# A two-layer decoder trunk: attention scores in plain fp32 on two halves of the array

## The chip, the core and the metric

The kernel runs on one core of one Trainium2 chip. The core has TensorE (matrix products; PE in the profile, its weight loads PEld), VectorE (DVE), ScalarE (ACT), GpSimd (POOL) and SyncE (SP), which here only issues DMAs. The engines run side by side, each through its own list of instructions, and wait for each other through semaphores. The metric is the device time of one execution in microseconds (us).

## The reference, cut to what matters

256 positions of width 1024 go through two layers. Layer 0 has three groups of heads of width 64 that read one input projection: sparse attention (8 heads, 2 key groups; compressed blocks, selected blocks and a window, mixed by gates), block attention (8 heads) and attention into 256 memory tokens (4 heads). Layer 1 has retention (4 heads) and again memory attention. Each group is gated, the groups are joined, projected back and added to the residual; a norm ends it. With 256 positions the selected blocks, the window and the block attention all come to plain causal attention:

```python
s = einsum('bqhd,bshd->bhqs', q, k) * HEAD_DIM ** -0.5
p = masked_softmax(s, causal)
o = einsum('bhqs,bshd->bqhd', p, v)
# compressed blocks: 15 per key group, each from 32 positions
hid = silu(einsum('bnlgd,lde->bnge', blocks + pe, w1))
kc_or_vc = einsum('bnge,ef->bngf', hid, w2)
```

## The kernel before, in words

Nearly all time goes into projections (`project`, `project_turned`, `project_mem`, `out_project`). Each weight slice of 128 x 1024 is loaded into a "raw" buffer and split by `split` (L102) into a high part (ScalarE, L106, type float32r) and the rest (VectorE, L107); the activations are split as well, and `mm3` adds three float32r products, L119 to L121.

Attention works on pairs of heads, hh = 0 and 1. The channels of the two heads lie on the partitions 0 to 63 and 64 to 127. For the scores, `stack_q` (L311) puts the high part of a head's queries on one half of the partitions and the rest on the other half, and `stack_k` (L318) does the like for keys with the high part on both halves (`dst`) and the rest on both halves (`lo`). `scores` then needs two float32r products over all 128 rows for one head (L372, L373). The scores lie in two PSUM banks "s" (`BANKS`, L25).

`causal_pair` (L398) does the softmax: VectorE adds the mask and takes the maximum (L405), ScalarE the exponential (L407), the sums are inverted and applied, TensorE transposes the probabilities (L178), ScalarE copies them to `pt` (L419). The value products are plain fp32: head hh writes the column half 64 hh to 64 hh + 63 of the bank `o`, first 256 columns for the first 128 keys (L421), then 128 columns for the rest (L423). `mem_attention` (L439) is the same with 256 memory keys and four products of 256 columns (L469). The profile shows each plain fp32 product as two records, each with its weight load. There are four sparse pairs with two branches each, four block pairs, and two memory attentions of two pairs.

In `compress` (L494) keys and values go one after the other through a hidden layer (16 products of 30 columns each, L530) that fills one column half. In `sparse_pair` (L577) the compressed values start the sum `o` with two products of 15 rows (L585).

The order on each engine comes from a scheduler that places instructions by priority as soon as, by its own estimate, their inputs and a buffer are there; the program gives the priority by its order. Buffers with one tag share a fixed number of slots: `tl("v4", shape, NV)` is one of 12 slots of 4 KB per partition. A tile gets a slot when an earlier tile with the tag has been read for the last time; where the slot is taken over, its first writer waits for that reader. In the last projection (`out_project(5, ys, True)`, L695) the four last weight slices are "late": their eight halves go into "v4" slots (L708) and are held until all five sums (four of 512, 512, 512 and 256 columns in "pj" and "tr", and `rest` of 256 in "s") have taken them in. At that time `x0` holds two "v4" slots (L725) and `gf` one (L837). The end (from L841) adds the residual to each sum (L854, L851), squares it (ScalarE, L856), multiplies by the gain (L858, L862), scales (L865, L866) and writes the output (L867, L868).

Of the kernel before, what the change touches and what calls it, by code (L numbers as in the profile page):

```python
# [21 lines left out]
NV = 12  # L22
# [29 lines left out]
def trunk(  # L52
# [33 lines left out]
    def load(t, src):  # L86
        nc.sync.dma_start(t, src)
        return t

# [221 lines left out]
    def stack_q(dst, src):  # L311

        for i in range(2):
            own, other = slice(64 * i, 64 * i + 64), slice(64 - 64 * i, 128 - 64 * i)
            S.copy(dst[own, :, i], src[own])
            V.tensor_tensor(dst[other, :, i], src[own], dst[own, :, i].bitcast(F32), ALU.subtract)

    def stack_k(dst, lo, src):  # L318

        for i in range(2):  # L320
            own, other = slice(64 * i, 64 * i + 64), slice(64 - 64 * i, 128 - 64 * i)
            S.copy(dst[own, :, i], src[own])
            V.tensor_copy(dst[other, :, i], dst[own, :, i].bitcast(F32))
            V.tensor_tensor(lo[own, :, i], src[own], dst[own, :, i].bitcast(F32), ALU.subtract)
            G.tensor_copy(lo[other, :, i], lo[own, :, i].bitcast(F32))

    def mem_query(ps, rb, dst):
        e = tl("tmp2", [P, 512], 3).rearrange("p (k t) -> p k t", k=2)
        scaled(ps, rb, 0.125, e)
        stack_q(dst, e)  # L330
# [13 lines left out]
    def heads_q(ps, plain=None):  # L344

        dst = [tl("v4", [P, 2, 2, T], NV, F32R) for _ in range(2)]

        def done(b, ts):
            for i in range(2):
                stack_q(dst[i][:, :, :, ts], b[:, 2 * i : 2 * i + 2])  # L350
            if plain is not None:
                S.copy(plain[:, :, ts], b)

        rot_transpose(ps, "q", done)
        return dst

    def heads_k(ps):
        dst = [tl("v4", [P, 2, 2, T], NV, F32R) for _ in range(2)]
        lo = [tl("v4", [P, 2, 2, T], NV, F32R) for _ in range(2)]

        def done(b, ts):
            for i in range(2):
                stack_k(dst[i][:, :, :, ts], lo[i][:, :, :, ts], b[:, 2 * i : 2 * i + 2])

        rot_transpose(ps, "k", done)
        return dst, lo
# [8 lines left out]
    def pair_scores(q, k, kl):  # L375

        out = []
        for hh in range(2):
            s = bank("s")
            for tok, a in enumerate(SPAN):  # L380
                scores(s[:, a], q[:, hh, tok * P : (tok + 1) * P], k[:, hh, : a.stop - a.start], kl[:, hh, : a.stop - a.start])
            out.append([s[:, a] for a in SPAN])
        return out

    def branch_scores(q, k, kl):


        s0 = bank("s").rearrange("p (h b n) -> p h b n", h=2, b=2)
        got = [[[None, None], [None, None]] for _ in range(2)]
        for hh in range(2):  # L390
            scores(s0[:, hh], q[:, hh, 0:P], k[:, hh, :, 0:P], kl[:, hh, :, 0:P])
            s1 = bank("s").rearrange("p (b n) -> p b n", b=2)
            scores(s1, q[:, hh, P:T], k[:, hh], kl[:, hh])
            for br in range(2):
                got[br][hh] = [s0[:, hh, br], s1[:, br]]
        return got

    def causal_pair(ss, v, gate, o, first, last):  # L398
# [11 lines left out]
        for hh in range(2):  # L410
# [8 lines left out]
            S.copy(pt[:, hh, :384], transposes([p[:, hh, i * P : (i + 1) * P] for i in range(3)]))  # L419
        for hh in range(2):  # L420
            PE.matmul(o[hh * 64 : hh * 64 + 64, 0:T], v(hh, 0), pt[:, hh, 0:T], start=first, stop=False)  # L421
        for hh in range(2):
            PE.matmul(o[hh * 64 : hh * 64 + 64, P:T], v(hh, 1), pt[:, hh, T : T + P], start=False, stop=last)  # L423
# [8 lines left out]
    def mem_keys(ps, rstd, rb, kT, kl, v):  # L432
        e = tl("tmp2", [P, 512], 3).rearrange("p (k t) -> p k t", k=2)
        scaled(ps[0], rb, 1.0, e)
        stack_k(kT, kl, e)
# [3 lines left out]
    def mem_attention(eqT, kT, kl, v, szT, y):  # L439
        for pr in range(2):  # L440
# [4 lines left out]
            sm = tl("sm", [P, 2, 2], 3)  # L445
            for hh in range(2):
                s = bank("s")
                for tok in range(2):
                    a, qs = slice(tok * T, (tok + 1) * T), slice(tok * P, (tok + 1) * P)
                    scores(s[:, a], eqT[:, pr, hh, qs], kT[:, pr, hh], kl[:, pr, hh])  # L450
# [38 lines left out]
    def sparse_queries():  # L489
        nonlocal qT, nq  # L490
        qT = tl("v4", [P, 4, T], NV)
        nq = heads_q(project(w512, W["nq"], (xh, xl)), qT)
# [144 lines left out]
    def block_queries():  # L637
        nonlocal mq
        mq = heads_q(project(w512, W["mq"], (xh, xl)))
# [331 lines left out]
```

## Time and profile before

| what | us |
|---|---|
| median of three runs | 450.48 (450.01 to 451.08) |
| the profiled execution, its own time | 450.25 |
| its span, first to last instruction | 448.5 |
| TensorE busy | 435.9 |
| VectorE busy | 331.7 |
| ScalarE busy | 257.3 |
| GpSimd busy | 9.4 |

The span is what the profile shows; the time of the execution is 1.8 us longer. "Busy" of TensorE counts an instruction from its start to its modelled end, and instructions overlap: a product of 512 columns has a length of 0.39 us and is followed by the next after 0.23. For prices one therefore reads the step from one start to the next. L178 is the transposes' line, L119 to L121 are the projections'.

### The profile page before, as it was taken

The page shows a single profiled execution, that of the slowest core. Times are in us where ns is not written, and L with a number is a line of the kernel's source. Part 1 is how long each engine was busy: PE and PEld are TensorE (multiplying, and loading weights), DVE is VectorE, ACT ScalarE, POOL GpSimd, SP SyncE. Part 2 cuts the span into 40 slices and gives each one's busy share as a digit, 9 for nine tenths or more (in the row PEclk, how much of TensorE's full clock was granted, in tenths as well). Part 3 has the DMA queues.
Part 4 walks back from the last instruction along what each step waited for, and adds up shares of the span by engine and source line. Part 5 has one row for each costly group of instructions (what it writes and reads, how often), then busy time and mean ns, then how long its engine had stood idle before and what let it go on. Part 6 is the DMA issues. An engine that isn't in the chain of part 4 may idle for free.

```text
span 448.5 us, 7101 instructions
## 1 busy us (share of the span) xinstructions
PE 435.9 (97%) x2586; PEld 367.8 (82%) x2586; DVE 331.7 (74%) x762; ACT 257.3 (57%) x472; POOL 9.4 (2%) x22
## 2 busy tenths in 40 slices
PE   8999999999999799999999999999999999999994
PEld 6988899888777467667999888888998888888883
DVE  4898989997888766756898776577877478764725
ACT  5756557947656966854646625464543356453714
POOL 0000100001101000000010000000000000000000
PEclk9999999999999999999999999999999999999998
DMA  8965765853343134222546334455545545555402
GB/s 281 391 227 185 214 235 176 274 187 134 102 142 132 56 117 165 95 94 95 176 145 214 142 117 166 164 178 160 190 145 186 187 142 203 159 209 198 142 0 94
DMA packets 22146, 74.20 MB, mean 165 GB/s; under 512 B 2720, under 2 KB 3424, under 8 KB 22112
## 3 DMA queue, kind: packets, MB, share of 16 engines
q1 hardware_dynamic: 21536, 72.92, 47.1%
q10 hardware_dynamic: 576, 0.84, 0.6%
q8 instruction: 20, 0.33, 0.3%
q14 instruction: 14, 0.11, 0.1%
HBM read 72.70 MB, written 1.05 MB: 164 GB/s over the span
## 4 chain that ended last, share of the span: by engine, by line
PE 91%; DVE 3%; ACT 3%; DMA 1%; issue 1%; ACTq 0%
PE pj L119 23%; PE pj L120 23%; PE pj L121 22%; PE t L178 3%; PE o L421 2%; PE s L372 1%; PE s L120 1%; PE s L119 1%; PE o L469 1%; PE s L121 1%; PE tr L120 1%; PE tr L119 1%; PE s L373 1%; PE tr L121 1%; DMA vec<-in_vec 1%
## 5 line engine op out<-in xcount | busy, mean ns | idle before, releaser
L107 DVE TENSOR_TENSOR wlo<-raw,whi 128x1024 fp32r<-128x1024 f32 (+2 forms) x124 | 145.1, 1174 | 58.2 <-ACT whi L106 57.2
L106 ACT CAST whi<-raw 128x1024 fp32r<-128x1024 f32 (+2 forms) x124 | 124.6, 1007 | 94.0 <-PE pj L121 28.0
L120 PE MATMUL pj<-wlo,big 128*128 128x512 f32 (+2 forms) x264 | 99.0, 375 | 0.1
L121 PE MATMUL pj<-whi,big 128*128 128x512 f32 (+2 forms) x264 | 98.3, 373 | 0.0
L119 PE MATMUL pj<-whi,big 128*128 128x512 f32 (+2 forms) x264 | 92.7, 376 | 0.0
L119 PE MATMUL pj<-big,whi 128*128 128x256 f32 x288 | 80.6, 285 | 0.7 <-ACT big L198 0.6
L120 PE MATMUL pj<-big,whi 128*128 128x256 f32 x288 | 81.1, 285 | 0.0
L121 PE MATMUL pj<-big,wlo 128*128 128x256 f32 x288 | 80.0, 285 | 0.5 <-DVE wlo L107 0.4
L120 PEld LDWEIGHTS pj<-wlo,big 128*128 128x128 f32 x264 | 49.7, 188 | 9.1 <-issue 0.8
L119 PEld LDWEIGHTS pj<-big,whi 128*128 128x128 f32 x288 | 54.7, 191 | 2.5 <-ACT big L198 1.0
L121 PEld LDWEIGHTS pj<-whi,big 128*128 128x128 f32 x264 | 49.7, 188 | 8.4
L119 PEld LDWEIGHTS pj<-whi,big 128*128 128x128 f32 x264 | 49.2, 188 | 8.4 <-issue 0.4
L120 PEld LDWEIGHTS pj<-big,whi 128*128 128x128 f32 x288 | 55.0, 191 | 0.8 <-issue 0.4
L121 PEld LDWEIGHTS pj<-big,wlo 128*128 128x128 f32 x288 | 54.3, 191 | 1.0 <-DVE wlo L107 0.9
L407 ACT ACTIVATE p<-p,mx 128x256 f32<-128x256 f32 (+1 forms) x48 | 21.4, 448 | 1.5 <-DVE mx L405 1.3
L178 PE MATMUL t<-cst,p 128*128 128x128 f32 x104 | 18.0, 281 | 1.0 <-ACT pt L419 0.6
L405 DVE CUSTOM_DVE_ANT_0 p<-s,cst 128x256 f32<-128x256 f32 (+1 forms) x48 | 14.6, 353 | 4.9 <-PE t L178 4.4
L419 ACT COPY pt<-t 128x384 f32<-128x384 f32 x24 | 11.5, 479 | 10.7 <-PE t L178 10.6
L178 PEld LDWEIGHTS t<-cst,p 128*128 128x128 f32 x104 | 11.8, 140 | 6.0 <-issue 3.3
L372 PE MATMUL s<-v,v 128*128 128x256 f32 (+2 forms) x48 | 14.7, 326 | 0.2 <-DVE mx L405 0.2
L120 PE MATMUL pj<-wlo,y 128*128 128x512 f32 x36 | 14.2, 396 | 0.0
L373 PE MATMUL s<-v,v 128*128 128x256 f32 (+2 forms) x48 | 13.4, 298 | 0.0
(292 smaller groups left out, 649.5 us busy)
## 6 DMA issues: line engine op xcount, KB each, us to landing
raw<-in_w SPq DMA_DIRECT2D x91, 512.0 KB, 3.8
raw<-in_wout SPq DMA_DIRECT2D x28, 512.0 KB, 3.6
v<-in_xtok SPq DMA_DIRECT2D x4, 512.0 KB, 6.2
raw<-in_w SPq DMA_DIRECT2D x4, 280.0 KB, 3.4
v<-in_w SPq DMA_DIRECT2D x2, 512.0 KB, 7.0
raw<-in_memT SPq DMA_DIRECT2D x2, 512.0 KB, 3.5
raw<-in_memtok SPq DMA_DIRECT2D x2, 512.0 KB, 4.6
v<-in_grow SPq DMA_DIRECT2D x2, 512.0 KB, 5.5
```

The source lines that it names most:

```text
L106: S.copy(hi, raw)
L107: V.tensor_tensor(lo, raw, hi.bitcast(F32), ALU.subtract)
L119: PE.matmul(ps, lh, rh, start=start, stop=False, skip_group_check=shared)
L120: PE.matmul(ps, lh, rl, start=False, stop=False, skip_group_check=shared)
L121: PE.matmul(ps, ll, rh, start=False, stop=stop, skip_group_check=shared)
L178: PE.transpose(b[:, i * P : (i + 1) * P], a, ident)
L372: PE.matmul(s, q, k, start=True, stop=False)
L373: PE.matmul(s, q, kl, start=False, stop=True)
L405: V.tensor_tensor_reduce(p[:, hh, a], ss[hh][tok], cpak[:, C_CAUSAL + a.start : C_CAUSAL + a.stop], -1.0, 3e38, ALU.add, ALU.min, mx[:, hh ...
L407: S.activation(p[:, hh, a], p[:, hh, a], AF.Exp, bias=mx[:, hh, tok : tok + 1], scale=-1.0, accum_out=sm[:, hh, tok : tok + 1])
L419: S.copy(pt[:, hh, :384], transposes([p[:, hh, i * P : (i + 1) * P] for i in range(3)]))
L421: PE.matmul(o[hh * 64 : hh * 64 + 64, 0:T], v(hh, 0), pt[:, hh, 0:T], start=first, stop=False)
```

## The change

Queries and keys are no longer split and stacked: `heads` copies them once in fp32, and `scaled` writes those of the memory attention. `pair_scores` computes the scores of the two heads in plain fp32, head 0 on the rows 0 to 63 of the array and head 1 on the rows 64 to 127, in turns, each head into its own bank "s". `side_by_side` records a list of products that keep their order; the first of them can be made to wait for another instruction. The value products go through it too, in the order head 0, head 1, head 0, head 1, and wait for the copy of the second head's probabilities. So do the 32 products of the compression's hidden layer, keys on the column half 0, values on the half 1. The compressed values are one product of 128 rows and 128 columns, whose weights are zero outside each head's 15 rows. The pool "v4" has 10 slots instead of 12, the pool "s2" 9 instead of 6.

```diff
-NV = 12
+NV = 10
+NS = 9
...
+    def after(ins, *others):
+        for other in others:
+            tc.add_manual_dep(ins.ins, other.ins.name,
+                              mybir.DependencyInfo(mybir.DependencyClass.Sync, mybir.DependencyReason.DATA), reason="pair")
+
+    def side_by_side(todo, *others):
+        for i, (out, lhs, rhs, start, stop) in enumerate(todo):
+            ins = PE.matmul(out, lhs, rhs, start=start, stop=stop)
+            if i == 0:
+                after(ins, *others)
+            else:
+                tc.keep_in_program_order(ins)
...
-    def heads_q(ps, plain=None):
-        dst = [tl("v4", [P, 2, 2, T], NV, F32R) for _ in range(2)]
...
+    def heads(ps, name):
+        dst = tl("v4", [P, 4, T], NV)
+        rot_transpose(ps, name, lambda b, ts: S.copy(dst[:, :, ts], b))
         return dst
...
-    def scores(s, q, k, kl):
-        PE.matmul(s, q, k, start=True, stop=False)
-        PE.matmul(s, q, kl, start=False, stop=True)
...
+    def pair_scores(q, k, spans):
+        s = [bank("s") for _ in range(2)]
+        side_by_side([(s[hh][:, a], q[pair_half(hh), tok * P : tok * P + P], k[pair_half(hh), : a.stop - a.start], True, True)
+                      for tok, a in enumerate(spans) for hh in range(2)])
+        return [[s[hh][:, a] for a in spans] for hh in range(2)], s
...
-            S.copy(pt[:, hh, :384], transposes([p[:, hh, i * P : (i + 1) * P] for i in range(3)]))
-        for hh in range(2):
-            PE.matmul(o[hh * 64 : hh * 64 + 64, 0:T], v(hh, 0), pt[:, hh, 0:T], start=first, stop=False)
-        for hh in range(2):
-            PE.matmul(o[hh * 64 : hh * 64 + 64, P:T], v(hh, 1), pt[:, hh, T : T + P], start=False, stop=last)
+            got = S.copy(pt[:, hh, :384], transposes([p[:, hh, i * P : (i + 1) * P] for i in range(3)]))
+        side_by_side([(o[hh * 64 : hh * 64 + 64, kt * P : T], v(hh, kt), pt[:, hh, kt * T : kt * P + T],
+                       first and kt == 0, last and kt == 1) for kt in range(2) for hh in range(2)], got)
...
+        vcR = tl("vcr", [P, 2, 2, 64])
+        G.memset(vcR, 0.0)
...
-            hb = bank("s")
-            for lp in range(16):
-                PE.matmul(hb[:64, :30], w1t[i][:, lp], blk[:, lp].rearrange("p g n -> p (g n)"),
-                          start=lp == 0, stop=lp == 15)
...
+        hb = bank("s")
+        side_by_side([(hb[64 * i : 64 * i + 64, :30], w1t[i][:, lp], blks[i][:, lp].rearrange("p g n -> p (g n)"),
+                       lp == 0, lp == 15) for lp in range(16) for i in range(2)], got)
...
-        for g in range(2):
-            n = 2 * pr + g
-            cr = slice(32 * (n % 4), 32 * (n % 4) + 15)
-            PE.matmul(o[g * 64 : g * 64 + 64, :T], vcR[cr, g], pcT[cr, n // 4], start=True, stop=False)
-        ss = branch_scores(nq[pr // 2][:, pr % 2], kS, kL)
+        PE.matmul(o[:, :T], vcR[:, pr % 2].rearrange("p g f -> p (g f)"), pcT[:, pr // 2], start=True, stop=False)
         for br in (1, 2):
-            causal_pair(ss[br - 1],
+            causal_pair(pair_scores(nq[:, pr], kS[:, br - 1], SPAN)[0],
```

The instructions move as follows. First TensorE at the block attention. Before (L372 and L373 are scores, L178 transposes, L421 the first value product, `o_1996` the sum it goes to; the `pj` rows are the output projection):

```order
L372 MATMUL s_2091<-v_190_1078,v_317_1748 128x128
L373 MATMUL s_2091<-v_192_1080,v_317_1748 128x128
L372 MATMUL s_2091<-v_190_1078,v_317_1748 128x256
L373 MATMUL s_2091<-v_192_1080,v_317_1748 128x256
L372 MATMUL s_2096<-v_190_1078,v_317_1748 128x128
L373 MATMUL s_2096<-v_192_1080,v_317_1748 128x128
L372 MATMUL s_2096<-v_190_1078,v_317_1748 128x256
L373 MATMUL s_2096<-v_192_1080,v_317_1748 128x256
L178 MATMUL t_2030<-cst_66,p_2007 128x128 x3
L421 MATMUL o_1996<-pt_2018,v_324_1785 64x256
L119 MATMUL pj_2143<-whi_2257,y_1948 128x512
L120 MATMUL pj_2143<-wlo_2258,y_1948 128x512
```

Behind the lone L421 stand eight rows of projections, and only then the pair's other value products. After (L100 is `side_by_side`: rows with `o` are value products, rows with `s` are scores):

```order
L100 MATMUL o_1852<-pt_1870,v_315_1688 64x256 x2
L100 MATMUL o_1852<-pt_1870,v_315_1688 64x128 x2
L194 MATMUL t_1917<-cst_66,p_1902 128x128 x3
L100 MATMUL s_1982<-v_183_1046,v_308_1665 128x128
L100 MATMUL s_1983<-v_183_1046,v_308_1665 128x128
L100 MATMUL s_1982<-v_183_1046,v_308_1665 128x256
L100 MATMUL s_1983<-v_183_1046,v_308_1665 128x256
L194 MATMUL t_1925<-cst_66,p_1902 128x128 x3
L135 MATMUL pj_2030<-whi_2144,y_1851 128x512
L136 MATMUL pj_2030<-wlo_2145,y_1851 128x512
```

The four value products of a pair stand together in two rows of two, and the scores of two heads alternate between two banks; each of the two groups has become one block.

Second, TensorE at the end of the program. `v_844` to `v_848` before, and `v_833` to `v_837` after, are halves of the late weight slices; `pj`, `tr` and `s` are the sums. Before:

```order
L120 MATMUL tr_4264<-v_842_4526,y_4175 128x256
L121 MATMUL tr_4264<-v_841_4525,y_4175 128x256
L119 MATMUL tr_4264<-v_844_4531,y_4175 128x256
L120 MATMUL tr_4264<-v_845_4532,y_4175 128x256
L121 MATMUL tr_4264<-v_844_4531,y_4175 128x256
L119 MATMUL tr_4264<-v_847_4537,y_4175 128x256
L120 MATMUL tr_4264<-v_848_4538,y_4175 128x256
L121 MATMUL tr_4264<-v_847_4537,y_4175 128x256
L121 MATMUL s_4541<-v_844_4531,y_4175 128x256
L119 MATMUL s_4541<-v_847_4537,y_4175 128x256
L120 MATMUL s_4541<-v_848_4538,y_4175 128x256
L121 MATMUL s_4541<-v_847_4537,y_4175 128x256
```

The sums of `pj` are closed at this point, and the last rows take in the last slice for `tr` and `s`. After:

```order
L135 MATMUL tr_4128<-v_836_4401,y_4039 128x256
L137 MATMUL s_4405<-v_833_4395,y_4039 128x256
L135 MATMUL s_4405<-v_836_4401,y_4039 128x256
L136 MATMUL pj_4125<-v_837_4402,y_4039 128x512
L137 MATMUL pj_4125<-v_836_4401,y_4039 128x512
L136 MATMUL pj_4126<-v_837_4402,y_4039 128x512
L137 MATMUL pj_4126<-v_836_4401,y_4039 128x512
L136 MATMUL pj_4127<-v_837_4402,y_4039 128x512
L137 MATMUL pj_4127<-v_836_4401,y_4039 128x512
L136 MATMUL tr_4128<-v_837_4402,y_4039 128x256
L137 MATMUL tr_4128<-v_836_4401,y_4039 128x256
L136 MATMUL s_4405<-v_837_4402,y_4039 128x256
```

The rows that use `v_837`, and with them the closing row of each of the five sums, have moved to the end.

Third, VectorE at the same place, with the engines that an instruction waits for. Before (`v_848` is the last late half, `wlo_4502` a later split, L854 the first addition of the residual):

```order
L107 TENSOR_TENSOR v_845_4532<-raw_4529,v_844_4531 128x1024 [waits DMAHW4_49,Activation_49]
L107 TENSOR_TENSOR wlo_4484<-raw_4481,whi_4483 128x1024 [waits DMAHW0_49,Activation_49]
L107 TENSOR_TENSOR v_848_4538<-raw_4535,v_847_4537 128x1024 [waits DMAHW5_49,Activation_49]
L107 TENSOR_TENSOR wlo_4502<-raw_4499,whi_4501 128x1024 [waits DMAHW1_49,Activation_49]
L854 TENSOR_TENSOR v_397_2137<-pj_4261,v_397_2137 128x512 [waits PE_49]
```

After (L123 is the split, L800 the addition):

```order
L123 TENSOR_TENSOR wlo_4348<-raw_4345,whi_4347 128x1024 [waits DMAHW1_49,Activation_49]
L123 TENSOR_TENSOR wlo_4366<-raw_4363,whi_4365 128x1024 [waits DMAHW2_49,Activation_49]
L123 TENSOR_TENSOR v_837_4402<-raw_4399,v_836_4401 128x1024 [waits DMAHW6_49,PE_49]
L800 TENSOR_TENSOR v_389_2024<-pj_4125,v_389_2024 128x512 [waits PE_49]
L800 TENSOR_TENSOR v_389_2024<-pj_4126,v_389_2024 128x512 [waits PE_49]
L804 TENSOR_TENSOR p_4470<-v_389_2024,v_779_4123 128x512 [waits DVE_49]
L800 TENSOR_TENSOR v_390_2026<-pj_4127,v_390_2026 128x512 [waits PE_49]
```

The split that writes `v_837` has become the last one and waits for TensorE (PE_49) where that of `v_848` waited for ScalarE; it takes the slot of `v_828`, whose last reader on TensorE is `tr_4128<-v_828`, eleven matmuls ahead of the first row that reads `v_837`. Behind it stand all additions of the end.

## Rows read from the trace of the kernel before

**Rows 1.** The page: busy us, share and instructions; the chain; one group (busy, mean, idle before).
```profile
PE 435.9 (97%) x2586; PEld 367.8 (82%) x2586; DVE 331.7 (74%) x762; ACT 257.3 (57%) x472; POOL 9.4 (2%) x22
...
PE 91%; DVE 3%; ACT 3%; DMA 1%; issue 1%; ACTq 0%
...
L121 PE MATMUL pj<-big,wlo 128*128 128x256 f32 x288 | 80.0, 285 | 0.5 <-DVE wlo L107 0.4
```

**Rows 2.** Timeline, TensorE, 198.5 to 202.5 us: start, length, line, out<-in, shapes, records.
```profile
198.31 0.39 PE L121 MATMUL pj<-whi,y 128*128 128x512 f32 x1
198.54 0.40 PE L121 MATMUL tr<-whi,y 128*128 128x512 f32 x1
198.87 0.43 PE L421 MATMUL o<-pt,v 128*64 128x256 f32 x1
198.88 0.43 PE L423 MATMUL o<-pt,v 128*64 128x128 f32 x2
...
199.66 0.55 PE L178 MATMUL t<-cst,p 128*128 128x128 f32 x3
...
201.26 0.65 PE L421 MATMUL o<-pt,v 128*64 128x256 f32 x2
201.83 0.50 PE L119 MATMUL pj<-whi,y 128*128 128x512 f32 x1
202.17 0.39 PE L120 MATMUL pj<-wlo,y 128*128 128x512 f32 x1
```

**Rows 3.** Timeline, TensorE, around 95.5 us: the compressed values.
```profile
95.18 0.28 PE L120 MATMUL pj<-big,whi 128*128 128x256 f32 x1
95.30 0.28 PE L121 MATMUL pj<-big,wlo 128*128 128x256 f32 x1
95.51 0.65 PE L585 MATMUL o<-s,vcr 15*64 15x256 f32 x4
96.09 0.55 PE L178 MATMUL t<-cst,p 128*128 128x128 f32 x3
```

**Rows 4.** Stretch table: length, busy us of PE, PEld, DVE, ACT, POOL; clock, DMA, GB/s.
```profile
144.00:157.00 13.00, 10.51 (x64) 6.47 (x63) 9.16 (x29) 12.30 (x40) 0.00 (x0) 1.00 0.25 82
```

**Rows 5.** Timeline, all engines, around 434.5 us and from 441.9 us on.
```profile
434.49 0.39 PE L121 MATMUL pj<-v,y 128*128 128x512 f32 x1
...
434.92 0.69 DVE L854 TENSOR_TENSOR v<-pj,v 128x512 f32<-128x512 f32 x1 [6.89 <-PE pj L121]
...
441.95 0.28 PE L121 MATMUL s<-v,y 128*128 128x256 f32 x1
...
443.98 0.16 DVE L864 RECIPROCAL ss<-ss 128x1 f32<-128x1 f32 x1 [0.16 <-ACT ss L863]
444.17 0.72 ACT L865 ACTIVATE p<-p,ss 128x512 f32<-128x512 f32 x1 [0.23 <-DVE ss L864]
444.18 0.49 DVE L866 TENSOR_SCALAR p<-p,ss 128x512 f32<-128x512 f32 x1
...
444.93 0.35 ACTq L867 DMA_DIRECT2D out_y<-p  x1
```

**Rows 6.** Timeline, TensorE, around 271 us: plain fp32 products in the full array.
```profile
270.59 1.03 PE L786 MATMUL s<-v,v 128*128 128x256 f32 x4
271.46 0.61 PE L788 MATMUL s<-v,v 128*128 128x128 f32 x4
```

**Rows 7.** Timeline, TensorE, around 64 us: the compression's first layer.
```profile
62.36 3.92 PE L530 MATMUL s<-tmp,v 128*64 128x30 f32 x64
66.20 0.39 PE L120 MATMUL pj<-big,whi 128*128 128x256 f32 x1
```

**Rows 8.** Timeline, TensorE, around 166.5 us: the scores of one block head.
```profile
166.32 0.22 PE L372 MATMUL s<-v,v 128*128 128x128 f32 x1
...
166.78 0.86 PE L121 MATMUL pj<-whi,ym 128*128 128x512 f32 x3
```

**Rows 9.** Groups by line and form, VectorE: count, busy us, mean ns, idle before.
```profile
L107 DVE TENSOR_TENSOR v<-raw,v 128x1024 fp32r<-128x1024 f32 x4 | 4.9, 1224 | 3.2 <-ACT v L106 3.2
```

More of the change, by code (lines that the diff above doesn't have):

```diff
@@ L309, in scaled, with pair_half @@
                                rb.unsqueeze(1).to_broadcast([P, 2, T]), op0=ALU.mult, op1=ALU.mult)
[L311 to L330, printed above, removed]
+    def pair_half(hh):
+        return slice(64 * hh, 64 * hh + 64)
     szn = tl("v4", [P, 4, T], NV)
@@ L342, in rot_transpose @@
             done(b.rearrange("p (k t) -> p k t", t=P), slice(tok * P, (tok + 1) * P))
-    def heads_q(ps, plain=None):
-        dst = [tl("v4", [P, 2, 2, T], NV, F32R) for _ in range(2)]
[L348 to L354, printed above, removed]
-        return dst
[L357 to L366, printed above, removed]
@@ L368, in trunk @@
-    SPAN = (slice(0, P), slice(P, 3 * P))
-    def scores(s, q, k, kl):
-        PE.matmul(s, q, k, start=True, stop=False)
-        PE.matmul(s, q, kl, start=False, stop=True)
-    def pair_scores(q, k, kl):
-        out = []
-        for hh in range(2):
[L379 to L383, printed above, removed]
@@ L445, in mem_attention @@
             sm = tl("sm", [P, 2, 2], 3)
+            _, ss = pair_scores(eqT[:, pr], kT[:, pr], WHOLE)
             for hh in range(2):
[L447 to L450, printed above, removed]
+                s = ss[hh]
                 V.tensor_reduce(mx[:, hh], s.rearrange("p (a k) -> p a k", a=2), AX.X, ALU.max, negate=True)
@@ L497, in compress @@
         w1t = [load(tl("v4", [P, 16, 64], NV), w1[i]) for i in range(2)]
-        w2t = load(tl("yf", [P, T], 2)[:64, :P], w2)
+        w2t = tl("yf", [P, T], 2)[:, :P]
+        for i in range(2):
+            load(w2t[64 * i : 64 * i + 64], w2)
         gates = tl("gates", [P, 2, 24])
@@ L532, in compress @@
[L532 to L549 removed]
+                    got = V.tensor_tensor(blk[l2 * 64 : (l2 + 1) * 64, :, g, :], src,
+                                          pe[gs, l2].unsqueeze(2).to_broadcast([64, 16, 15]), ALU.add)
@@ new lines, in compress @@
+            blks.append(blk)
+        hb = bank("s")
+        side_by_side([(hb[64 * i : 64 * i + 64, :30], w1t[i][:, lp], blks[i][:, lp].rearrange("p g n -> p (g n)"),
+                       lp == 0, lp == 15) for lp in range(16) for i in range(2)], got)
+        h = tl("hid", [P, 30])
+        S.activation(h, hb[:, :30], AF.Exp, scale=-1.0)
+        V.tensor_scalar(h, h, 1.0, None, op0=ALU.add)
+        V.reciprocal(h, h)
+        V.tensor_tensor(h, hb[:, :30], h, ALU.mult)
+        for g in range(2):
+            V.tensor_copy(srep[:, g, :, :15], h[64:, g * 15 : (g + 1) * 15].unsqueeze(1).to_broadcast([64, 4, 15]))
@@ new lines, in compress @@
+        PE.matmul(hb[:64, 64:94], w2t[:64, 0:64], h[:64], start=True, stop=True)
+        for g in range(2):
+            PE.matmul(hb[:, 128 + g * 64 : 192 + g * 64], srep[:, g].rearrange("p a b -> p (a b)"),
+                      w2t[64:, 64:128], start=True, stop=True)
+        for g in range(2):
+            S.copy(kcBD[g * 64 : (g + 1) * 64, g * 15 : (g + 1) * 15], hb[:64, 64 + g * 15 : 79 + g * 15])
+        for a in range(4):
+            rows = slice(32 * a, 32 * a + 15)
+            S.copy(vcR[rows, a // 2, a % 2], hb[rows, 128 + 64 * (a % 2) : 192 + 64 * (a % 2)])
@@ L556, in compressed_scores @@
                 c = (tok * 4 + pr) * 30
-                PE.matmul(s[:, c : c + 30], qT[:, pr, tok * P : (tok + 1) * P], kcBD, start=True, stop=True)
+                PE.matmul(s[:, c : c + 30], nq[:, pr, tok * P : (tok + 1) * P], kcBD, start=True, stop=True)
         sc = tl("sc", [P, 2, 8, 15])
```

123 lines of the change are left out of this document (42 added, 81 removed).

## The prediction

> **What bounds the kernel now.** First the page's list of engines and its chain that ended last: TensorE is busy for 97% of the span and 91% of the chain is TensorE's own instructions [rows 1]. So a stage is worth what TensorE spends in it, and time on another engine counts only where TensorE waits for that engine. A busy TensorE is no TensorE at its peak, though, so I read starts and not durations: TensorE's rows one by one, where the step from one start to the next is the price of the first. A float32r product of 512 columns steps by 0.23 us [rows 2], one of 256 columns by 0.12 [rows 3]; their weight loads are hidden. A plain fp32 product appears as two records. The stretch table then shows the one place where TensorE is not the limit: between 144 and 157 us ScalarE is busy 12.30 of 13 us and TensorE 10.51 [rows 4]. The last rows show the end: 6.4 us from the end of the last matmul (441.95 plus 0.12) to the end of the span at 448.5 [rows 5]. The granted clock is at its upper level, 2.4 GHz, in that stretch (1.00) [rows 4].
>
> **What the change costs, part by part.** Times are set against the profiled execution, 450.25 us (span 448.5); the median of the three runs shown is 0.23 us above it.
>
> *Value products.* There are 16 groups of four products: 4 sparse pairs in two branches and 4 block pairs make 12 groups of 256, 256, 128, 128 columns, and the two memory attentions make 4 groups of four times 256. Before, 11 of the 12 and 3 of the 4 were pulled apart: one product alone, later the other three. One pair shows both [rows 2]. Three together: hh1's 256 columns (198.87) and hh0's 128 (198.88) start within 0.01 us of each other, and all of it takes 0.79 us until the next load starts (199.66). Alone: 0.57 us (201.26 to 201.83). Around it lies the change of array shape: the product at 198.54 holds TensorE 0.33 instead of 0.23, and the one at 201.83 holds it 0.34, as its load is no longer hidden. So a lone product costs 0.57 + 0.10 + 0.11 = 0.78 us between projections, somewhat less beside transposes; I take 0.75. In the new order all four stand together, and each column half carries 256 and then 128 columns, just what hh1's half carried in the 0.79: the lone excursion disappears. 14 x 0.75 = **-10.5 us**. Bounds: nothing, if the fourth product should add its own 0.57 to the group, up to -11.
>
> *Compressed values.* Four excursions of two products on 15 rows become one product of 128 rows and 128 columns. Before: 0.58 (95.51 to 96.09), plus 0.09 that the product at 95.30 holds longer than 0.12 [rows 3]. After: two fp32 products of 256 columns in the full array take 0.87 (270.59 to 271.46), so 0.43 each, with no change of shape around them [rows 6]. 4 x 0.24 = **-1.0 us**.
>
> *Hidden layer of the compression.* 64 records in 3.84 us (62.36 to 66.20), all in one column half [rows 7]; now the two networks alternate on both halves. No row shows so short products side by side; the nearest are the two loads and starts at 198.87, by which two share one step [rows 2]: **-1.8 us**. The other end is 0.
>
> *Scores.* Before, with stacked operands in the full array: a block head takes 0.46 (166.32 to 166.78) [rows 8], so 8 x 0.46 = 3.7; sparse 16 x 0.23 + 16 x 0.12 = 5.6; memory 32 x 0.12 = 3.8; together 13.1. After, each of 16 groups is an excursion into row halves. If the halves work side by side as column halves do, a group of 128 and 256 columns per half costs the 0.79 [rows 2], plus 0.05 for loading 128 columns of weights instead of 64 (an estimate: half the 0.11 that an exposed load costs at 201.83), plus 0.10 and 0.09 around it: 1.03. A memory group has 256 twice: 0.21 more, 1.24. 12 x 1.03 + 4 x 1.24 = 17.3; three groups are pulled apart in the new order, at 0.3 each: 18.2. **+5.1 us.** No row shows two products on different rows and the same columns. Nearest for side by side: two products on different rows (and different columns) that take the time of one [rows 3]. Nearest for one after the other: the full array's fp32 products [rows 6]. That end adds, at 0.43 for 256 columns and half for 128, 12 x 0.64 + 4 x 0.86 = 11.1 us. I take side by side, since two column halves already stream different data at once.
>
> *The copies.* 48 splits and copies of queries and keys leave VectorE, 36 leave ScalarE and all 14 GpSimd; 7 wide copies on ScalarE come. TensorE's own work covers nearly all of it. I count **-0.4 us**, what TensorE waits for VectorE's weight splits in the costliest group that has such a wait [rows 1]. Bounds: -3, if ScalarE's relief at 144 to 157 us is felt in full [rows 4], and +4.0, the third rival.
>
> *The end.* The pool "v4" shrinks from 12 to 10 buffers. At the end x0 holds two, the final gain one, and the last four weight slices eight: eleven. The order shows what follows: the last slice's lower half (v_837) now waits for TensorE before VectorE may write it, as it takes over the buffer of v_828, and the ten matmuls that close the five sums stand at the very end, where before four of the five sums closed one after another while TensorE went on. v_828's last reader stands eleven matmuls ahead of the ten; they take 1.3 us at 0.12. The split that waits for that reader takes 1.22 us [rows 9] and starts 0.3 to 0.4 us after the reader's start: TensorE stands still for some 0.4 us. Then from the start of the last ten: the first sum closes at 0.23, VectorE takes it up 0.43 later (434.49 to 434.92), and has before it eight operations of 0.69, one of half the columns (0.42, an estimate), two of 0.49 and five small ones of some 0.16, with gaps 8.0 us in all; ScalarE's last scaling, 0.72 beside VectorE's 0.49, ends 0.25 later, and from the output DMA's issue to the end it is 3.6 (444.93 to 448.5) [rows 5]: 12.4 us, of which TensorE's ten matmuls are 1.9. The tail is 10.5 us instead of 6.4. **+4.5 us** with the stall. Late next in place of TensorE is VectorE, which had done tok 0's half before.
>
> Sum: -10.5 - 1.0 - 1.8 + 5.1 - 0.4 + 4.5 = -4.1: 446.15, with the 0.23 to the median **446.4 us**.
>
> **Rivals.** *One: the row halves take turns.* Place: the 16 score groups. Price +11.1, so 457.5, slower; from 4.1 of the 11.1 (37% not hidden) the change stops being a gain. For it: no row shows it otherwise, and both halves end in the same columns. Against: column halves, and corners of the array, do work side by side [rows 2, 3]. 12%.
>
> *Two: the tail is covered after all* (the closing order costs nothing). Then 441.9. Against: the buffer count and the waits in the order are fixed before the run. 7%.
>
> *Three: what TensorE saves from 144 us on comes back as waiting.* Eight split groups lie there (6.0 us), minus 2.0 us more for scores: 4.0 saved, while ScalarE sets the pace at 144 to 157. If all of it returns, 450.4: no change. For it: ScalarE's 12.30 of 13 us [rows 4]. Against: ScalarE loses copies there too, and from 164 us on projections fill the gaps. 22%.
>
> *Four: weight loads are not hidden within a half.* Each group then has three loads more in the open, 0.11 each (the price at 201.83): 16 x 0.33 = 5.3, so 451.7. Against: the product at 198.54 follows at 0.23 although its weights went to the same rows of the array [rows 2], and four fp32 records with four loads take 0.87 [rows 6]. 4%. The Trainium skill, "TensorE: Matmul & The Clock Gate", Part 3 (The mechanism), says that a weight load overlaps running matmuls only where the row group differs. By that rule the time is this rival's; the steps of 0.23 and 0.87 speak against it.
>
> **How the numbers follow.** Forecast 55%, rivals 12, 7, 22 and 4. A measurement of this kernel can tell about 0.2% (0.9 us) from no change: faster is below 449.6, slower above 451.4. The forecast's own range, 443 to 450, gives faster 52 of its 55, same 3; rival two gives 7 faster; rival three, spread from 448 to 453, gives 9 faster, 8 same, 5 slower; rivals one and four give 16, all but 1 slower. Faster 0.68, same 0.12, slower 0.20. The range 442.5 to 452 leaves out rival one, most of rival two and the edges.
>
> **What will show it.** Value groups: four products within 0.8 us, no lone excursion. Scores: a pair's two products start within 0.02 us and the group takes near 0.85; 1.5 would be rival one. Compressed values about 0.43. The compression's 64 records in about 1.9 us. At the end a wait of TensorE near 0.4 us for VectorE's split, then five closing sums within 2 us and some 10.5 us to the end of the span. Waits of TensorE at 144 to 207 us near their present size; twice that is rival three. I am wrong if the score groups cost over 0.25 us more each than said, or if the tail is as before.

## The result, and the profile after

The changed kernel takes 444.81 us (median of 4 runs, 444.80 to 444.96) against 450.25 us: the ratio is 0.9875, with a 95% interval of 0.9860 to 0.9891. That is 5.4 us faster. The forecast was 446.4 us, 4.1 us faster by its own sum; the time lies within the range. All line numbers below are those of the kernel that is being told of.

The page of the changed kernel: busy time, and the chain that ended last.

```profile
PE 427.0 (96%) x2610; PEld 361.5 (82%) x2610; DVE 308.8 (70%) x712; ACT 245.7 (55%) x445; POOL 1.9 (0%) x9
...
PE 95%; DVE 2%; ACT 1%; DMA 1%; issue 0%; ACTq 0%
```

TensorE's busy time fell by 8.9 us, from the 435.9 of [rows 1] to 427.0. The span fell by 5.5, from 448.5 to 443.0. The rest, 3.4 us, has to be waiting or the end.

First the groups of products. Timeline of the changed kernel, TensorE: the compression's hidden layer, a value group of the memory attention (L100, o), a score group (L100, s) and the compressed values (L534).

```profile
61.21 2.06 PE L100 MATMUL s<-tmp,v 128*64 128x30 f32 x64
63.19 0.39 PE L137 MATMUL pj<-big,wlo 128*128 128x256 f32 x1
...
155.81 0.40 PE L137 MATMUL tr<-whi,ym 128*128 128x512 f32 x1
156.13 1.08 PE L100 MATMUL o<-pt,s 128*64 128x256 f32 x8
157.15 0.55 PE L194 MATMUL t<-cst,p 128*128 128x128 f32 x3
...
157.62 0.93 PE L100 MATMUL s<-v,v 64*128 64x128 f32 x8
158.48 0.70 PE L534 MATMUL o<-s,vcr 128*128 128x256 f32 x2
159.02 0.49 PE L194 MATMUL t<-cst,p 128*128 128x128 f32 x3
```

Read the starts. The 64 records of the hidden layer take 1.98 us (61.21 to 63.19) instead of 3.84 [rows 7]. The eight records of a value group stand in one row of the timeline, 1.02 us for four products of 256 columns; before, such a group came as one product and later three, as in [rows 2]. The eight records of a score group take 0.86 us, and one by one they start 7 ns apart in pairs (0, 7, 213, 220, 325, 332, 543 and 550 ns): both row halves run at once. Rival four would leave the later weight loads in the open. The Trainium skill, "TensorE: Matmul & The Clock Gate", Part 3 (The mechanism), has its rule in a list (a weight load overlaps running matmuls only where the row group differs), but names a background weight buffer as well in the text above it. The trace disagrees with the rule: the first load of 0.107 us and the passes of 0.107, 0.107, 0.214 and 0.214 are 0.75, and the last 0.1 of the 0.86 lies behind the last pass, before the next load, as it does at a change of array shape elsewhere (155.81 to 156.13 is 0.32 us for a product that steps by 0.23 among its like). So no later load costs anything.

Then the end. Timeline of the changed kernel, all engines: v_837's split, the stall, the ten closing products and what follows them.

```profile
429.83 1.23 DVE L123 TENSOR_TENSOR v<-raw,v 128x1024 fp32r<-128x1024 f32 x1 [10.94 <-PE tr L136]
...
430.70 0.28 PE L135 MATMUL s<-v,y 128*128 128x256 f32 x1
431.11 0.19 PEld L136 LDWEIGHTS pj<-v,y 128*128 128x128 f32 x1 [0.34 <-DVE v L123]
431.11 0.50 PE L136 MATMUL pj<-v,y 128*128 128x512 f32 x1
...
432.97 0.28 PE L137 MATMUL s<-v,y 128*128 128x256 f32 x1
433.08 0.68 DVE L804 TENSOR_TENSOR p<-v,v 128x512 f32<-128x512 f32 x1
433.68 0.68 DVE L800 TENSOR_TENSOR v<-pj,v 128x512 f32<-128x512 f32 x1
434.28 0.68 DVE L800 TENSOR_TENSOR v<-tr,v 128x512 f32<-128x512 f32 x1
...
438.97 0.35 ACTq L813 DMA_DIRECT2D out_y<-p  x1
```

The split waits for TensorE (<-PE tr), TensorE waits for the split (<-DVE v L123, a step of 0.41 instead of 0.12), and VectorE then works off both halves, one operation each 0.60 us. From the last product's step (432.97 plus 0.12) to the end of the span it is 9.9 us, against 6.4 before [rows 5].

### The profile page after: what moved, and what is told of

Its sections match the earlier page's. It is cut to its first block, busy times and chain, and to the rows that moved or that the text cites. A ratio compares the mean times of both kernels' runs of the same rounds, so it can differ in the third digit from the quotient of the medians.

```text
span 443.0 us, 7033 instructions
## 1 busy us (share of the span) xinstructions
PE 427.0 (96%) x2610; PEld 361.5 (82%) x2610; DVE 308.8 (70%) x712; ACT 245.7 (55%) x445; POOL 1.9 (0%) x9
## 3 DMA queue, kind: packets, MB, share of 16 engines
HBM read 72.73 MB, written 1.05 MB: 167 GB/s over the span
## 4 chain that ended last, share of the span: by engine, by line
PE 95%; DVE 2%; ACT 1%; DMA 1%; issue 0%; ACTq 0%
PE pj L135 24%; PE pj L136 24%; PE pj L137 24%; PE s L100 4%; PE t L194 4%; PE o L100 3%; PE tr L136 1%; PE s L135 1%; PE s L136 1%; PE s L137 1%; PE tr L135 1%; PE tr L137 1%; DMA vec<-in_vec 1%; PE s L732 1%; PE tr L194 1%; DVE v L800 1%
## 5 line engine op out<-in xcount | busy, mean ns | idle before, releaser
L123 DVE TENSOR_TENSOR wlo<-raw,whi 128x1024 fp32r<-128x1024 f32 (+2 forms) x124 | 145.1, 1173 | 72.8 <-ACT whi L122 71.9
L367 ACT ACTIVATE p<-p,mx 128x128 f32<-128x128 f32 (+1 forms) x48 | 21.3, 447 | 3.1 <-DVE mx L365 3.1
L365 DVE CUSTOM_DVE_ANT_0 p<-s,cst 128x128 f32<-128x128 f32 (+1 forms) x48 | 14.3, 354 | 5.2 <-PE t L194 5.1
L123 DVE TENSOR_TENSOR v<-raw,v 128x1024 fp32r<-128x1024 f32 x4 | 4.9, 1226 | 14.7 <-PE tr L136 10.9
L135 PE MATMUL pj<-whi,y 128*128 128x512 f32 x36 | 13.4, 408 | 1.0 <-ACT y L387 1.0
```

Of the source, the lines that this page charges most:

```text
L123: V.tensor_tensor(lo, raw, hi.bitcast(F32), ALU.subtract)
L135: PE.matmul(ps, lh, rh, start=start, stop=False, skip_group_check=shared)
L365: V.tensor_tensor_reduce(p[:, hh, a], ss[hh][tok], cpak[:, C_CAUSAL + a.start : C_CAUSAL + a.stop], -1.0, 3e38, ALU.add, ALU.min, mx[:, hh ...
L367: S.activation(p[:, hh, a], p[:, hh, a], AF.Exp, bias=mx[:, hh, tok : tok + 1], scale=-1.0, accum_out=sm[:, hh, tok : tok + 1])
```

## The experiments

A name that begins with b is the kernel before with a part of the change; one that begins with a (and copies_pinned) is the changed kernel with something altered. The table holds all twelve: the median; TensorE's busy time (page); and from the stretch table TensorE's idle time in 36 to 128, 128 to 160 and 160 to 207 us (length less busy time), and the granted clock at 128 to 160 us.

| kernel | us | ratio to before (95%) | PE busy | idle 36-128 | 128-160 | 160-207 | clock |
|---|---|---|---|---|---|---|---|
| before | 450.25 | | 435.9 | 0.57 | 2.85 | 0.85 | 1.00 |
| after | 444.81 | 0.986-0.9891 | 427.0 | 0 | 2.44 | 1.61 | 1.00 |
| a_end | 440.86 | 0.9782-0.9826 | 426.7 | 0 | 2.44 | 1.61 | 1.00 |
| a_headwise | 450.69 | 0.9991-1.0015 | 432.6 | 0 | 2.09 | 2.18 | 1.00 |
| b_values | 443.10 | 0.9828-0.9853 | 425.7 | 0.55 | 3.72 | 2.77 | 0.95 |
| b_comp | 451.80 | 1.0025-1.0053 | 434.3 | 0.57 | 4.71 | 0.89 | 1.00 |
| b_all_but_scores | 445.09 | 0.9877-0.9908 | 426.1 | 0.56 | 6.05 | 2.75 | 0.89 |
| b_scores | 455.18 | 1.0101-1.0131 | 443.2 | 0 | 0.79 | 0.57 | 1.00 |
| a_end_copies | 448.16 | 0.9941-0.9967 | 433.2 | 1.31 | 0.93 | 1.62 | 1.00 |
| a_end_sparse | 447.66 | 0.9929-0.9961 | 427.5 | 0.58 | 5.85 | 2.53 | 0.95 |
| a_late_memory | 443.77 | 0.9831-0.9876 | 430.0 | 0 | 2.54 | 0.80 | 0.95 |
| a_early_memory | 442.40 | 0.9802-0.9848 | 427.4 | 0.16 | 0 | 2.95 | 1.00 |
| b_early_memory | 449.29 | 0.9961-1.0005 | 428.4 | 3.82 | 1.57 | 5.86 | 1.00 |
| copies_pinned | 463.88 | 1.0294-1.0322 | 435.0 | 10.69 | 1.36 | 4.72 | 1.00 |

Median and profile are not the same execution. Where the profiled one lies further from its median, it took 449.95 us (a_headwise), 450.76 (b_comp), 446.82 (a_end_sparse) and 440.97 (a_early_memory).

### a_end: the end by itself

The last two of the four kept weight slices go to buffers of the tag "big", which x1's halves have left by then.

```diff
...
-                wh, wl = split(raw, 1024, "v4" if late else None)
+                wh, wl = split(raw, 1024, "big" if late and i == total - 1 else "v4" if late else None)
```

> The changed kernel (444.8 us), with the last two of the four kept weight slices put into a tag whose buffers are free by then, so that no split waits for a closing matmul. Only the end of the order moves: four of the five sums close one after another again, as before the change. Forecast's theory (the end costs the changed kernel 4.5 us, by its trace 3.5 to 4.0): 440.3 to 441.3 us, and 6.4 us from the last matmul to the end of the span. Rival two (the tail is covered, the end costs nothing): 444.8.

Measured: 440.86 us, 3.95 less than the changed kernel. Timeline of a_end, the last product and the last output DMA; the span ends at 439.1.

```profile
432.49 0.28 PE L137 MATMUL s<-big,y 128*128 128x256 f32 x1
...
435.46 0.35 ACTq L813 DMA_DIRECT2D out_y<-p  x1
```

The tail is 6.5 us again (432.49 plus 0.12 to 439.1) and the idle times and the clock of the earlier stages are the changed kernel's to the hundredth. So the end cost some 3.95 us (the five executions lie between 440.5 and 443.4), rival two is out, and by its median this is the fastest kernel of all that were run.

### b_values and b_all_but_scores: the savings with the old scores kept

The first has only side_by_side for the value products (L421 and L423 of before become one call, L469 likewise); the second has in addition the one product for the compressed values and the alternated hidden layer, so that the scores alone (with their pools and their end) are missing from the change.

```diff
-        for hh in range(2):
-            PE.matmul(o[hh * 64 : hh * 64 + 64, 0:T], v(hh, 0), pt[:, hh, 0:T], start=first, stop=False)
...
+        side_by_side([(o[hh * 64 : hh * 64 + 64, kt * P : T], v(hh, kt), pt[:, hh, kt * T : kt * P + T],
+                       first and kt == 0, last and kt == 1) for kt in range(2) for hh in range(2)], got)
```

> The kernel before (450.25 us) with one part of the change alone: the four value products of a pair stand together. Theory (14 lone excursions at 0.75 us): 439.7 us, groups of 0.80 us body, nothing else changed. Rival (the group must wait until the second head's copy is there, and TensorE stands still for it where before it had a triple to do): half of it comes back, about 445.

> The kernel before (450.25 us) with all of the change but the scores and what belongs to them (float32r stacked queries and keys kept, pool of 12): value products together, compressed values as one product, hidden layer alternated. Theory (-10.5 -1.0 -1.8): 436.9 us, the fastest so far, because the new scores cost 5.1 and the end 4.5. Rival (the 98 copies that the new scores take off VectorE, ScalarE and GpSimd were what let the other parts pay; with them kept, ScalarE holds TensorE up at 144 to 157 us): 440 to 443.

Measured: 443.10 and 445.09 us; 7.1 and 5.1 us faster than before where 10.5 and 13.3 were expected; the first lies between its two expectations, the second is slower than both of its. The saving itself is there: in b_values TensorE's busy time fell by 10.2 us. A part of it came back as idle time (7.04 us from 36 to 207 us instead of 4.27), and a part of the busy time is spent at a lower clock. Stretch table of b_all_but_scores:

```profile
128.00:160.00 32.00, 25.95 (x145) 0.89 0.21 67
160.00:207.00 47.00, 44.25 (x258) 1.00 0.41 135
```

And its timeline in that stretch, where the input projections have run out and only attention is left:

```profile
140.11 0.28 PE L388 MATMUL s<-v,v 128*128 128x256 f32 x1
140.23 0.28 PE L389 MATMUL s<-v,v 128*128 128x256 f32 x1
141.86 0.61 PE L194 MATMUL t<-cst,p 128*128 128x128 f32 x3 [1.35 <-DVE p L434]
143.04 1.39 PE L100 MATMUL o<-pt,s 128*64 128x256 f32 x8 [0.57 <-ACT pt L435]
...
145.48 0.41 PE L388 MATMUL s<-v,v 128*128 128x256 f32 x1
145.70 0.41 PE L389 MATMUL s<-v,v 128*128 128x256 f32 x1
```

TensorE waits for VectorE (1.35) and ScalarE (0.57), and after the waits the same product steps by 0.22 us (145.48 to 145.70) instead of 0.12 (140.11 to 140.23): the clock has gone from 2.4 to 1.2 GHz. Account for b_all_but_scores: idle time from 36 to 207 us is 9.36 instead of 4.27, 5.1 us more; and 25.95 us at a mean 0.89 cost about 2.9 us (an estimate: 25.95 times 0.11). Together that is 8.0 of the 8.2 us that are missing.

### b_comp and b_scores: two parts alone

b_comp is the kernel before with the compression's two edits (the diff's compress() and the one product in sparse_pair), b_scores the kernel before with the new scores, their pools and a_end's end. The "slow fifth variant" of the text is b_all_but_scores.

> The kernel before (450.25 us) with the compression alone changed: compressed values as one product, hidden layer alternated on both column halves. Theory of the forecast (each term is TensorE time and arrives whole): -1.0 -1.8, so 447.4 us. Rival, formed after the first four runs (the order that the scheduler makes decides how much attention is left when the input projections have run out, and TensorE waits and its clock falls there; in this kernel's order 48 rows of attention stand behind the last input projection, 32 in the kernel before, 17 in the changed one, 45 in the slow fifth variant): the 2.8 saved are given back and more, 450 to 453, with over 4 us of waiting and a clock below 1.00 between 130 and 157 us.

> The kernel before (450.25 us) with the scores alone changed (plain fp32, alternated, no stacked operands), its pool of 10 and the last weight slices in free buffers so that the end stays as it was. Theory of the forecast (+5.1 for the groups, -0.4 for the copies): 455.0 us. Rival (run-out: only 17 rows of attention stand behind the last input projection instead of 32, so most of the 2.9 us of waiting at 144 to 164 us goes): 452 to 453.

Measured: 451.80 and 455.18 us. The compression alone makes the kernel slower by 1.7 us although its 64 records went from 3.85 to 1.99 us. Its profiled execution, the shortest of seven, shows where the saving went: busy time fell by 1.6 us and idle time at 128 to 160 us went up by 1.9. That accounts for 0.5 of the 1.7 us; for the rest there is no profile, only a lower mean clock (0.990 to 0.994 in the other six, 0.997 here). The rival's time and its wait of over 4 us came true, its low clock did not: 1.00 with 4.71 us of idle time, where b_values shows 0.95 with 3.72. So the sum of the waits in a stretch doesn't tell what the clock does. The scores alone cost 5.1 us, near the 4.7 that the forecast's theory had for them, but by another road: TensorE is busy for 7.3 us more and idle for 2.9 us less between 36 and 207 us. With all the rest in place, the same scores are a gain: 445.09 without them (b_all_but_scores), 440.86 with them (a_end). **The parts do not add up.** Alone the first three are worth -7.1, +1.7 and +5.1; with the +4.0 of the end, which was measured in the changed kernel, that makes +3.7. As a whole the change is worth -5.4.

### a_headwise: is it the alternation that makes the halves run at once?

```diff
-                      for tok, a in enumerate(spans) for hh in range(2)])
+                      for hh in range(2) for tok, a in enumerate(spans)])
```

> The changed kernel (444.8 us) with a pair's score products issued head by head (both of the first head, then both of the second) instead of alternately; nothing else. Theory (the two row halves run at once only where a product of one stands next to a product of the other, since TensorE takes them in order): in a group of 128 and 256 columns the second head starts with the first head's last record, at 0.43 us, so the body is 1.19 instead of 0.86 us; memory groups 1.60 instead of 1.07; 12 x 0.33 + 4 x 0.54 = 6.1, so 450.9 us. Rival (each half works off its own queue, the order does not matter): 444.8.

Measured: 450.69 us, 5.9 more than the changed kernel, as the theory said, and yet the theory is wrong. Timeline of a_headwise: a group that the scheduler cut between the heads (87.16 and 89.07), and one that stayed together, the same as the one at 157.62 above; the last row is the same group asked for up to 160.3 us only:

```profile
87.16 0.92 PE L100 MATMUL s<-s,v 64*128 64x128 f32 x4
88.01 0.66 PE L194 MATMUL t<-cst,tmp 128*128 128x128 f32 x4
...
89.07 0.92 PE L100 MATMUL s<-s,v 64*128 64x128 f32 x4
89.92 0.50 PE L136 MATMUL pj<-wlo,big 128*128 128x512 f32 x1
...
160.19 0.93 PE L100 MATMUL s<-v,v 64*128 64x128 f32 x8
161.05 0.70 PE L534 MATMUL o<-s,vcr 128*128 128x256 f32 x2
...
160.19 0.39 PE L100 MATMUL s<-v,v 64*128 64x128 f32 x2
```

The second takes 0.86 us as in the changed kernel. Record by record, the second head's first product (128 columns) starts 13 ns after the first head's, and the first head's second product (256 columns), which is written before it, starts 0.31 us later: the last row holds two starts of 128 columns within its 0.39 us. A group that stays together doesn't mind the order. What costs is that the scheduler cut six of the sixteen groups between the heads: each head then needs 0.85 us alone (87.16 to 88.01, 89.07 to 89.92) and a change of array shape of its own, six times some 1.05 us. The changed kernel has four groups that are cut, but in the alternated order a cut leaves at most one product of each head without its partner. The lone heads show rival one's price, too: one half takes as long as both together.

### a_end_copies and copies_pinned: the copies by themselves

Both are a_end with the removed copies put back as scratch work of the old shapes and number on VectorE, ScalarE and GpSimd; nothing reads what they write. In the second, TensorE's order is pinned to a_end's.

```diff
...
+            S.copy(a.bitcast(F32R), src[own])
+            V.tensor_tensor(b.bitcast(F32R), src[own], cst_like(own, src.shape), ALU.subtract)
...
```

> The fastest so far (440.9 us: the changed kernel with the free end) with the load of the removed copies put back on VectorE, ScalarE and GpSimd, as copies of the old shapes and number into scratch that nothing reads; the scores don't use them. 14 rows of attention stand behind the last input projection, as few as without. Theory A (the engines' load by the copies is what made the variants with stacked operands wait): 443.5 to 445 us, and waits of TensorE at 144 to 157 us that grow by 3 us. Theory B (the order is what counts, the copies are covered): 440.9 to 441.5.

> The kernel with the removed copies put back as scratch work (448.2 us, against 440.9 without them), with TensorE's instructions pinned to the order that they have in the kernel without the copies; in the unpinned one 606 of 2407 matmuls stood in another place. Order theory (the scheduler reacts to the copies with an order that pulls groups apart, and that order is what costs): 441 to 442.5 us, with about 0.6 more waiting at 36 to 56 us, as in the kernel before. Load theory (VectorE and ScalarE are too late with the copies, in whatever order): 444.5 to 449, with waits at 128 to 207 us that are 3 us or more above those of the kernel without copies.

Measured: 448.16 and 463.88 us, 7.3 and 23.0 more than a_end. Neither theory named such sizes. In the first, the idle time of 36 to 207 us is even a little less than a_end's (3.86 against 4.05); it is busy time that grew, by 6.5 us: the scheduler had reacted to the copies with 27 stretches of score products instead of 20. With the order pinned there are 20 again, and TensorE waits. Waits of TensorE in copies_pinned, in total, times and longest:

```profile
PE tr L201 <- DVE junk L344: 12.8, 3, 6.2
PE o L107 <- ACT pt L415: 2.3, 1, 2.3
```

Transposes into "tr", a tag of one bank, wait until VectorE's copies have read the bank's last content. So the order theory fell: with the order kept, the copies cost three times as much. The load theory has the right sign but not the place: it looked for the waits at 128 to 207 us, where they grew by 2.0, while TensorE was idle for 10.69 us at 36 to 128 us, nearly all of it at that one bank. (In a pinned order TensorE cannot do other work during such a wait.) The clock counts too: 0.93 at 36 to 128 us, and busy time is 8.3 us above a_end's with the same order. The copies are no exact double of the old ones (no score waits for them, and GpSimd's, which wait for nothing, all ran in the first 36 us), so 7.3 and 23.0 are not the price of the old ones.

### a_end_sparse: stacked scores for the sparse pairs only

```diff
-            causal_pair(pair_scores(nq[:, pr], kS[:, br - 1], SPAN)[0],
+        ss = branch_scores(nq[pr // 2][:, pr % 2], kS, kL)
+            causal_pair(ss[br - 1],
```

> The same fastest kernel (440.9 us) with the scores of the sparse pairs alone as before the change: stacked float32r operands for their keys and queries, the rest in plain fp32. By the terms, TensorE saves 8 x 1.03 - 5.6 = 2.6 us: 438.3 us if the terms simply add. Theory B (run-out: 33 rows of attention stand behind the last input projection here instead of 17): the 2.6 are given back as waiting between 135 and 157 us, 440.5 to 443.

Measured: 447.66 us, 6.8 more than a_end, worse than both numbers. Idle time at 128 to 160 us is 5.85 us instead of 2.44, the clock 0.95. It looks like b_all_but_scores, with about a quarter of the copies (12 of 48 on VectorE) and with the changed kernel's pools. So neither the number of copies nor the pools alone set the waits.

### a_late_memory, a_early_memory, b_early_memory: only the order of the stages

The last theory to be tried was that the waits follow from the order: how much attention is left when the input projections have run out. Only the calls at the end of layer 0's definitions move, in the two early ones like this:

```diff
     compressed_scores()
-    block_gates()
-    block_keys()
     memory_rows()
-    for pr in range(3):
-        sparse_pair(pr)
+    sparse_pair(0)
     memory_scale()
     memory_keys()
     memory_group()
+    sparse_pair(1)
+    sparse_pair(2)
+    block_gates()
+    block_keys()
...
```

> The changed kernel with the free end (440.9 us), the same instructions, the stages of layer 0 written in another order: block queries and values before the second and third sparse pair, the memory group and the last sparse pair last. Of the attention, 68 matmuls then stand behind the last input projection instead of 35. Run-out theory (waits and a clock below 1.00 grow with what stands behind the last projection, whichever scores are used): 443.5 to 446 us, with 5 to 7 us of waiting at 128 to 160 us instead of 2.4. Theory A (the copies of the stacked operands are what costs): 440.9, since there are none here.

> The same kernel (440.9 us) with the memory stages written right after the compressed scores and the first sparse pair, so that the first output projection has its first rows early: the longest stretch without a projection is 29 matmuls instead of 35. Run-out theory: a part of the 4.0 us of waiting at 128 to 207 us goes, 438 to 440.5. Theory A: 440.9.

> The variant with stacked float32r scores and all the rest of the change (445.1 us), in the same new order of stages; the longest stretch without a projection is 36 matmuls instead of 79. Run-out theory: the forecast's terms arrive (-10.5 -1.0 -1.8), 436 to 439 us, the fastest of all, because the plain scores cost TensorE 5 us more. Theory A (98 copies on the other engines): 443 or more, whatever the order.

Measured: 443.77, 442.40 and 449.29 us. The first was slower than a_end by 2.9 us, as the run-out theory's number said, but not by waiting (3.34 us idle against 4.05, and 2.54 at 128 to 160 us where 5 to 7 were expected): its busy time grew by 3.3, in part at a low clock, 0.58 at 148 to 152 us. The second was to be faster than a_end and was 1.5 us slower, which the scatter of its executions (440.97 to 444.75) doesn't rule out as chance; it had no idle time left at 128 to 160 us and 2.95 at 160 to 207: the waits moved on. The third, which was to be the fastest, was slower than b_all_but_scores by 4.2, as theory A had it (443 or more): its 6.05 us at 128 to 160 became 1.57, but 3.82 and 5.86 appeared on either side. Its executions scatter from 446.5 to 452.8. Timeline of b_early_memory, TensorE, and its stretch table:

```profile
67.67 3.26 PE L100 MATMUL s<-tmp,v 128*64 128x30 f32 x62 [1.27 <-DMA v<-in_w]
...
70.00:74.00 4.00, 4.00 (x30) 0.50 0.78 267
```

Of the 3.82 us, 1.7 (1.27 of them here) are waits for the DMA that brings the weights of the compression's hidden layer, and from 70 to 74 us TensorE runs at its lower level, 1.2 GHz (0.50). Over 36 to 128 us the clock is 0.94, which by the same estimate as above costs 5.3 us. So this run is no clean test of what it was made for. The order of the stages alone moved these kernels by up to 4.2 us, and in the first two the length of the last stretch without projections didn't tell how the waits would change. That theory is out as a rule for prediction.

## Why the prediction was right, and where it was not

**Bound, and rivals one, two and four: right.** TensorE was the bound and stayed it. Rival one is out (0.86 us for both halves), rival two (a_end, 3.95 us), rival four (no load in the open).

**Value products, -10.5.** Together they take 13.75 us after against 23.00 before (the steps of their 128 records), and stand in 16 stretches instead of 30. With some 0.2 us of change of shape for each of the 14 that are gone (a product of 512 columns ahead steps by 0.32 and one behind by 0.34, instead of 0.23), that is 12.0. b_values shows 10.2 of busy time. The size was right.

**Compressed values -1.0, hidden layer -1.8.** Steps: 2.31 to 1.65 us, with the changes of shape some 1.5 less; and 3.85 to 1.99. The mechanisms were right, the first gain was half as much again.

**Scores +5.1: right by luck.** Old 15.1 us by steps, not 13.1. New 16.6, and 4.0 for 20 stretches with some 0.2 us of change of shape around each: 20.6, not 18.2. Four groups were pulled apart, not three. So +5.5: both sides were set too low by 2.0 and 2.4 us, and the errors cancel. b_scores doesn't confirm the term: behind its +5.1 stand 7.3 us more busy time and 2.9 us less waiting. (By these steps the four terms make -9.9; TensorE's busy time fell by 8.9.)

**The end +4.5.** Measured 3.95; the mechanism is the one foretold. VectorE's operations follow one another at 0.60 us, not at the 0.69 and a gap that the working took, and the stall was 0.3 us instead of 0.4. (The working's terms from the start of the last ten add up to 12.5, not 12.4.)

**The copies -0.4: right as a number, wrong as a step.** The forecast took each part as TensorE time that arrives whole, with the waits as they were, and priced the copies by one wait for VectorE's weight splits in the kernel before. The waits did stay (4.27 us between 36 and 207 us before, 4.05 after), so the sum came out. But the runs show that they stay only where the new scores go with the other parts: with the old scores kept, the same savings brought 5.1 us more idle time and an estimated 2.9 us of clock (b_all_but_scores), more than the +4.0 that the forecast gave as the upper bound of this term. That the sum of single terms met the whole was luck. In company, plain scores with all that they remove are worth -4.2 us, not +4.7. Rival three, that the saved time comes back as waiting, is what happened in part or in whole in b_values, b_comp, b_all_but_scores and a_end_sparse. Its "against", that ScalarE loses copies too, may be why it didn't happen here; no run shows that, and I had given it a half sentence and no price.

**What stays open.** By which of their effects the plain scores hold the waits down: the load on VectorE and ScalarE, the hold on the one "tr" bank (shown only for scratch copies, in a pinned order), or the order that the scheduler makes of it. The order of the stages alone moves up to as much, and no run separates the three for the real copies.

## What to carry to other kernels

Where one engine is the bound and a scheduler fills its gaps, price a change as a whole: time saved on the bound engine arrives only as far as the others keep up, so ask of each part what it takes off them, and don't take the sum of parts tried one by one (+3.7 here) for the whole (-5.4). An expected number that comes out is no proof of its mechanism: a_headwise hit within 0.3 us for a reason that its own timeline refutes, and a_late_memory lay in a range whose waits it doesn't have. Look at which buffers the last work of the kernel needs; moving two slices to free ones was worth 3.95 us beside the change's own 5.4.

## What the runs showed of the hardware that was not expected

Products on different row halves of the array did not keep the order in which they were issued: in a_headwise the second head's first product starts 13 ns after the first head's first, ahead of a product written before it. And after the waits of 1.35 and 0.57 us that the rows of b_all_but_scores show, the clock fell from 2.4 to 1.2 GHz for some microseconds (256 columns step by 0.22 us instead of 0.12), so that a wait there costs more than its length; in the changed kernel, idle for 2.44 us in the same stretch, and in b_comp, idle for 4.71, it stayed at its upper level (1.00).
